# Two PSUM rows, an earlier fold and a whole load in the tail of a 2-D prefix-sum kernel

One Trainium2 chip, one core of it. The metric is the device time of one execution in microseconds (us); lower is better. A difference counts as faster or slower from 2% on.

## The reference

```python
def reference(x):                      # x: 4 x 4224 x 4224, float32
    ps = np.cumsum(np.cumsum(x, axis=1), axis=2)
    diag = np.diagonal(ps, axis1=1, axis2=2)
    return np.cumsum(diag, axis=1).astype(np.float32)
```

The output is small (4 x 4224), but every element of x above or below a diagonal place counts for some result, so all 285 MB have to be read.

## The kernel before

The kernel streams x in groups of 384 rows (three rows in each of 128 partitions, 6336 KB a load) through three buffers. ScalarE (ACT) sums rows left of the diagonal, VectorE (DVE) adds rows into column sums `u`, and TensorE (PE) gathers the column sums into a PSUM tile `d`. The last 384 rows of the last image come in two parts: part a (256 rows, two loads) and part b (128 rows, five small loads), so that little is left to do when the last bytes land. The change lies in this tail, and in how the group called 8 of the last image is loaded.

```python
# last image, groups 8 and 9: three loads each
for i, g in enumerate((LG - 2, LG - 1)):
    strip = strip_tile()
    for q in range(F):
        load(out=strip[:, q, :], in_=rows_of(b, g)[:, q, :])
    # ... act_sum and pair_sum of row sums, masked block, matmuls into d
    add_to(rsum[:, k, :], more[:, i, :])
# ...
matmul(carry_ps, earlier, pu, start=True)
matmul(carry_ps[:, 1:2], apart, pu[:, 0:1])
if not whole:
    sum_a(1, cp, c1, cp + 768)                     # part a, first piece: ACT and DVE
    for c in range(c0, cp, 256):                   # 768 columns folded to 256 by PE
        matmul(fold_a, ident, part_a[:, :, c : c + 256], start=c == c0)
# ... two scans on DVE, write-out of the other groups
sum_a(3, *acuts[1], acuts[1][0] + 640)             # part a, second piece
row_sums(asum[:, :, 5], fold_a)                    # "the fold": DVE reads PSUM
row_sums(arows, asum)
# ...
weigh_b(dtot[:, 2:3], weights, M0, start=True)     # fin_b: places 256 to 383
for h in range(2):
    weigh_a(arows[:, h : h + 1], h * P, start=h == 0)      # fin_a: places 0 to 255
for h in range(2):
    weigh_b(arows[:, h : h + 1], weights, h * P)
for k, ca in ((0, 416), (1, 416), (2, 416)):       # part b: ACT and DVE, three quarters
    act_sum(bsum[:, k, 0:1], part_b[:, k, :ca])
    pair_sum(bsum[:, k, 1:2], part_b[:, k, ca:])
    if k == 1:
        finish(fin_a, 0, M0)                       # yl = fin_a + c12
# ... weigh_b of bsum, three sums of the last quarter (esum), their matmuls (fin_e)
finish(fin_b, M0, GW)
# ... yl written out; ye = fin_e + yl, written out
```

In the code, `arows` holds the finished row sums of part a, the operand of its weighted sums `fin_a` and `fin_b`; `yl` and `ye` are the last outputs. Each engine takes its instructions in this order.

Of the kernel before, what the change touches and what calls it, by code (L numbers as in the profile page):

```python
# [8 lines left out]
FP32 = mybir.dt.float32  # L9
# [8 lines left out]
def kernel(  # L18
# [17 lines left out]
    nc = tc.nc  # L36
# [3 lines left out]
    P = 128  # L40
    F = 3
    GW = P * F
    NG = N // GW
    LB = B - 1
    LG = NG - 1
# [13 lines left out]
    psum_s = ctx.enter_context(  # L59
        tc.tile_pool(name="psum_s", bufs=1, space=bass.MemoryType.PSUM)  # L60
    )
# [6 lines left out]
    src = x[LB, T0:N, :].rearrange("(h p) w -> p h w", p=P)  # L68
# [4 lines left out]
    def strip_tile():  # L73
        return strips.tile([P, F, N], FP32, name="strip")

    def rows_of(b, g):

        return x[b, g * GW : (g + 1) * GW, :].rearrange("(p f) w -> p f w", f=F)

    load = nc.gpsimd.dma_start  # L80
# [17 lines left out]
    for um, pattern, cm in (  # L98
# [5 lines left out]
            out=um,  # L104
            in_=um,
# [12 lines left out]
        out=ident,  # L118
        in_=ident,
# [6 lines left out]
    def counted(name, rows, width, pieces):  # L126

        ti = consts.tile([P, GW], I32, name="counted")[:rows, :width]
        for c0, c1, base, step, cm in pieces:
            nc.gpsimd.iota(  # L130
                ti[:, c0:c1],
                pattern=[[step, c1 - c0]],
                base=base,
                channel_multiplier=cm,
            )
        tf = consts.tile([rows, width], FP32, name=name)
        nc.gpsimd.tensor_copy(out=tf, in_=ti)
        return tf
# [6 lines left out]
    def between_groups(name, n, turned):  # L145
# [37 lines left out]
    weights = counted("weights", P, GW, [(0, GW, 1, 1, -1)])  # L183
    nc.gpsimd.affine_select(
        out=weights,
        in_=weights,
# [8 lines left out]
    R = P // 4  # L195
# [3 lines left out]
        out=steps, in_=steps, scalar=2, op=ALU.arith_shift_right  # L199
    )  # L200
    weights4 = consts.tile([P, P], FP32, name="weights4")
    nc.vector.tensor_scalar_max(out=weights4, in0=steps, scalar1=0.0)

    def matmul(o, lhsT, rhs, start=False):
        nc.tensor.matmul(  # L205
            o, lhsT=lhsT, rhs=rhs, start=start, stop=False, skip_group_check=True
        )

    def act_sum(acc, src):

        nc.scalar.activation(out=src, in_=src, func=ACT.Copy, accum_out=acc)  # L211

    def row_sums(acc, src):
        nc.vector.reduce_sum(out=acc, in_=src, axis=AX.X)  # L214

    def pair_sum(acc, src):

        w = src.shape[-1] // 2
        pair = dumpool.tile([P, 896], FP32, name="pair")
        nc.vector.scalar_tensor_tensor(  # L220
            out=pair[:, :w],
            in0=src[:, :w],
            scalar=1.0,
            in1=src[:, w:],
            op0=ALU.mult,
            op1=ALU.add,
            accum_out=acc,
        )

    def add_to(o, i):  # L230
        nc.vector.tensor_add(out=o, in0=o, in1=i)  # L231

    def masked(o, i, m, acc):
        nc.vector.scalar_tensor_tensor(  # L234
            out=o,
            in0=i,
            scalar=1.0,
            in1=m,
            op0=ALU.mult,
            op1=ALU.mult,  # L240
            accum_out=acc,
        )
# [10 lines left out]
    asum = last.tile([P, 2, 6], FP32, name="asum")  # L253
    dtot = last.tile([P, F], FP32, name="dtot")
# [13 lines left out]
    for b in range(B):  # L268
        whole = b < LB
        if b in (0, LB):  # L270
            rows = NG if b else NW
# [4 lines left out]
        def row_of(j):  # L276
            return b * NG + j if whole else (j + 1) % NG

        def columns(j, rhs):

            k = row_of(j)
            matmul(d, sel[:, NW - 1 - k : NW - 1 - k + rows], rhs, start=first[0])
            first[0] = False

        def u_of(j):
            return u[:, j * GW : (j + 1) * GW]

        for g in range(NG if whole else LG - 2):
            strip = prefetched.pop(0) if prefetched else None
            if strip is None:  # L290
                strip = strip_tile()
                load(out=strip, in_=rows_of(b, g))  # L292
            k, lo, hi = row_of(g), g * GW, (g + 1) * GW
# [16 lines left out]
        if not whole:  # L310


            for j in range(LG - 2, NG):
                columns(j, u_of(j))
            columns(LG, head[:, 0, :])
            more = last.tile([P, 2, F], FP32, name="more")
            wa = 2176
            for i, g in enumerate((LG - 2, LG - 1)):
                k, lo, hi = row_of(g), g * GW, (g + 1) * GW
                strip = strip_tile()  # L320
                for q in range(F):
                    load(out=strip[:, q, :], in_=rows_of(b, g)[:, q, :])  # L322
                for q in range(F):
                    act_sum(rsum[:, k, q : q + 1], strip[:, q, :wa])
                    pair_sum(more[:, i, q : q + 1], strip[:, q, wa:hi])
                    block = strip[:, q, lo:hi]
                    masked(block, block, um3[:, q, :], rabove[:, k, q : q + 1])
                    for j in range(g + 1, NG):
                        columns(j, strip[:, q, j * GW : (j + 1) * GW])
                    columns(g, block)  # L330
                add_to(rsum[:, k, :], more[:, i, :])
# [8 lines left out]
        if not whole:  # L340

            strip = strip_tile()
# [7 lines left out]
            for sb, c0, c1 in (  # L350
# [6 lines left out]
                r0 = TB + sb * R  # L357
                load(  # L358
                    out=part_b[:, sb, c0:c1],
                    in_=x[b, r0 : r0 + R, :NH].rearrange("r (k c) -> r k c", k=4)[  # L360
                        :, :, c0:c1
                    ],
                )

            def sum_a(k, c0, c1, ca):
                for h in range(2):
                    act_sum(asum[:, h, k : k + 1], part_a[:, h, c0:ca])
                for h in range(2):
                    pair_sum(asum[:, h, k + 1 : k + 2], part_a[:, h, ca:c1])


            c0, c1 = acuts[0]
            cp = c0 + 768
            fold_a = psum_s.tile([P, 2, 256], FP32, name="fold_a")
# [3 lines left out]
        c12 = last.tile([rows, 2, GW], FP32, name=f"c12{rows}")  # L378
# [12 lines left out]
        for i, src in enumerate((d, c12[:, 0, :])):  # L391
            nc.vector.tensor_tensor_scan(  # L392
                out=c12[:, i, :],
# [6 lines left out]
        if whole:  # L400
# [5 lines left out]
            out=out[b, :T0].rearrange("(g i) -> g i", i=GW), in_=c12[1:, 1, :]  # L406
        )


        sum_a(3, *acuts[1], acuts[1][0] + 640)  # L410
        row_sums(asum[:, :, 5], fold_a)
        arows = last.tile([P, 2], FP32, name="arows")
        row_sums(arows, asum)


        M0 = 2 * P
        E0 = GW - R
        fin_a = psum_s.tile([1, M0], FP32, name="fin_a")
        fin_b = psum_s.tile([1, P], FP32, name="fin_b")
        fin_e = psum_s.tile([1, R], FP32, name="fin_e")  # L420
        yl = last.tile([1, GW], FP32, name="yl")

        def weigh_a(rows, r0, start=False):

            matmul(fin_a[:, r0:], rows, weights[:, : M0 - r0], start=start)

        def weigh_b(rows, w, r0, start=False):
            lo = max(r0, M0)
            matmul(fin_b[:, lo - M0 :], rows, w[:, lo - r0 : GW - r0], start=start)

        def finish(src, c0, c1):
            nc.vector.tensor_add(
                out=yl[:, c0:c1], in0=src, in1=c12[0:1, 1, c0:c1]
            )

        weigh_b(dtot[:, 2:3], weights, M0, start=True)
        for h in range(2):
            weigh_a(arows[:, h : h + 1], h * P, start=h == 0)
        for h in range(2):
            weigh_b(arows[:, h : h + 1], weights, h * P)  # L440


        bsum = last.tile([P, 3, 2], FP32, name="bsum")
        for k, ca in ((0, 416), (1, 416), (2, 416)):
            act_sum(bsum[:, k, 0:1], part_b[:, k, :ca])
            pair_sum(bsum[:, k, 1:2], part_b[:, k, ca:])
            if k == 1:
                finish(fin_a, 0, M0)
        for k in range(3):
            for i in (1, 0):  # L450
                weigh_b(bsum[:, k, i : i + 1], weights4, M0 + k * R)


        esum = last.tile([P, 3], FP32, name="esum")
# [2 lines left out]
        pair_sum(esum[:, 2:3], part_b[:, 3, bcut:])  # L457
        for k in (1, 0, 2):
            matmul(fin_e, esum[:, k : k + 1], weights4[:, :R], start=k == 1)
        finish(fin_b, M0, GW)  # L460
        nc.sync.dma_start(
            out=out[b, T0 : T0 + E0].unsqueeze(0), in_=yl[:, :E0]
        )
# [33 lines left out]
```

## Time and profile before

| | before |
|---|---|
| median of the first three runs, us | 670.92 (670.73 to 671.5) |
| span of the profiled run, us | 669.8 |
| bytes moved, mean rate | 285.61 MB, 426 GB/s |
| busy: PE, DVE, ACT | 13%, 67%, 40% |
| mean granted PE clock | 0.908 |

The DMA queue is full for the whole span, so only the few microseconds after the last landings can be shortened. The mean granted clock turns out to be worth reading: one stretch of 3.41 us at half clock lowers it by 3.41 x 0.5 / 669.8 = 0.0025. The mean granted PE clock of 0.908 is 119.4 us at half clock (from 523.5 to 642.9) and one stretch of 3.41 us in the tail.

### The profile page before, as it was taken

To read this page: it belongs to the slowest core of one execution; us is meant where nothing else is said; L and a number is where in the kernel's file an instruction comes from. 1 tells how busy PE (TensorE), PEld (TensorE's weight loads), DVE (VectorE), ACT (ScalarE), POOL (GpSimd) and SP (SyncE) were. 2 spreads that over 40 slices of the span, in tenths; PEclk is the share of its full clock that TensorE was granted. 3 is DMA by queue.
4 is the path that set the end of the run, shared out by engine and by line. 5 is a ranking of instruction groups with operands and counts; after the bars stand their busy time and mean duration, and the time that the engine had idled before them with its cause. 6 is when DMAs were issued, how large, how long until landed. Compare 5 with 4: busy or idle time off the path is not lost.

```text
span 669.8 us, 1147 instructions
## 1 busy us (share of the span) xinstructions
PE 84.9 (13%) x174; PEld 16.4 (2%) x174; DVE 450.1 (67%) x287; ACT 264.9 (40%) x251; POOL 36.1 (5%) x83
## 2 busy tenths in 40 slices
PE   0000110000010110000001000000002011000085
PEld 0000000000000000000000000000000000000022
DVE  3779866544398877655437988765442999876555
ACT  0012344556602333445661223344566122334743
POOL 5000000000000000000000000000000000000020
PEclk9999999999999999999999999999999655555588
DMA  9999999999999999999999999999999999999996
GB/s 371 436 436 436 436 436 436 430 436 433 433 427 418 430 436 436 433 433 436 436 433 436 436 433 436 436 424 418 427 436 436 430 436 436 436 436 416 425 423 266
DMA packets 8155, 285.61 MB, mean 426 GB/s; under 512 B 904, under 2 KB 1332, under 8 KB 1876
## 3 DMA queue, kind: packets, MB, share of 16 engines
q0 software_dynamic: 7680, 284.89, 98.7%
q1 hardware_dynamic: 468, 0.66, 0.3%
q14 instruction: 6, 0.05, 0.0%
q8 instruction: 1, 0.02, 0.0%
HBM read 285.47 MB, written 0.07 MB: 426 GB/s over the span
## 4 chain that ended last, share of the span: by engine, by line
DMA 66%; ACT 16%; DVE 14%; issue 2%; PE 1%; POOL 0%; ACTq 0%; DVEq 0%; POOLq 0%
DMA strip<-in_x_dram 66%; ACT strip L211 16%; DVE u L231 5%; DVE u L303 3%; DVE strip L300 2%; DVE above L214 2%; DVE sums L214 1%; PE d L205 0%; PE fin_b L205 0%; DVE c L392 0%; PE fin_a L205 0%; DVE pair L220 0%; POOL strip L347 0%; ACTq L211 0%; DVE asum L214 0%
## 5 line engine op out<-in xcount | busy, mean ns | idle before, releaser
L211 ACT ACTIVATE strip<-strip 128x768 f32<-128x768 f32 (+13 forms) x125 | 259.3, 2075 | 400.4 <-DMA strip<-in_x_dram 374.8
L231 DVE TENSOR_TENSOR u<-u,strip 128x3840 f32<-128x3840 f32 (+10 forms) x115 | 292.2, 2541 | 2.7
L300 DVE TENSOR_TENSOR strip<-strip,um 128x1152 f32<-128x1152 f32 x41 | 55.7, 1358 | 183.1 <-ACT strip L211 182.9
L205 PE MATMUL d<-u,sel 128*33 128x384 f32 (+1 forms) x88 | 64.6, 844 | 575.7 <-DVE u L231 575.7
L214 DVE TENSOR_REDUCE above<-strip 128x3 f32<-128x1152 f32 x41 | 55.5, 1353 | 1.4
L292 POOL DMA_DIRECT2D strip<-in_x_dram x38 | 20.2, 530 | 560.2 <-DVE u L231 504.2
L205 PEld LDWEIGHTS d<-u,sel 128*33 128x33 f32 (+1 forms) x88 | 8.0, 136 | 629.9 <-DVE u L231 626.9
L211 ACT ACTIVATION_READ_ACCUMULATOR strip<-strip 128x1 f32 x125 | 23.3, 186 | 0.0
L303 DVE TENSOR_TENSOR u<-strip 128x4224 f32<-128x4224 f32 x4 | 18.2, 4549 | 0.0
L220 DVE SCALAR_TENSOR_TENSOR pair<-strip 128x640 f32<-128x640 f32 (+6 forms) x15 | 9.8, 657 | 8.8 <-DMA strip<-in_x_dram 8.6
L205 PE MATMUL d<-strip,sel 128*11 128x384 f32 x30 | 10.0, 486 | 0.6 <-DVE strip L234 0.6
L214 DVE TENSOR_REDUCE sums<-strip 128x3 f32<-128x1152 f32 x4 | 5.4, 1341 | 7.0 <-DMA strip<-in_x_dram 7.0
L198 DVE TENSOR_SCALAR steps<-steps 128x128 int32<-128x128 int32 x1 | 0.2, 227 | 7.0 <-POOL steps L197 7.0
L322 POOL DMA_DIRECT2D strip<-in_x_dram x6 | 3.1, 529 | 27.4 <-issue 27.4
L214 DVE TENSOR_REDUCE pu<-d 33x1 f32<-33x384 f32 (+1 forms) x2 | 1.1, 548 | 3.6 <-PE d L205 3.6
L234 DVE SCALAR_TENSOR_TENSOR strip<-strip,um 128x384 f32<-128x384 f32 x6 | 3.3, 558 | 0.2
L358 POOL DMA_DIRECT2D strip<-in_x_dram x5 | 2.7, 552 | 4.9 <-DMA strip<-in_x_dram 4.9
L205 PE MATMUL fold_a<-strip,ones_all 128*128 128x512 f32 x6 | 2.8, 610 | 0.8 <-DMA strip<-in_x_dram 0.8
L205 PEld LDWEIGHTS d<-strip,sel 128*11 128x11 f32 x30 | 2.7, 93 | 7.7 <-issue 6.0
L205 PE MATMUL d<-ones_all,r 128*33 128x128 f32 (+1 forms) x12 | 2.3, 346 | 0.1
L347 POOL DMA_DIRECT2D strip<-in_x_dram x2 | 1.4, 709 | 13.2 <-issue 13.2
L392 DVE TENSOR_TENSOR_SCAN c<-ones_all,carry,c 33x384 f32<-33x384 f32 (+1 forms) x2 | 2.0, 1008 | 0.1
(73 smaller groups left out, 36.9 us busy)
## 6 DMA issues: line engine op xcount, KB each, us to landing
strip<-in_x_dram POOLq DMA_DIRECT2D x41, 6336.0 KB, 27.7
strip<-in_x_dram POOLq DMA_DIRECT2D x6, 2112.0 KB, 22.3
strip<-in_x_dram POOLq DMA_DIRECT2D x1, 2304.0 KB, 18.9
strip<-in_x_dram POOLq DMA_DIRECT2D x1, 1536.0 KB, 22.0
strip<-in_x_dram POOLq DMA_DIRECT2D x3, 480.0 KB, 23.1
head<-in_x_dram SPq DMA_DIRECT2D x1, 576.0 KB, 3.9
strip<-in_x_dram POOLq DMA_DIRECT2D x1, 352.0 KB, 23.8
strip<-in_x_dram POOLq DMA_DIRECT2D x1, 128.0 KB, 19.3
```

Of the source, the lines that this page charges most:

```text
L205: nc.tensor.matmul(o, lhsT=lhsT, rhs=rhs, start=start, stop=False, skip_group_check=True)
L211: nc.scalar.activation(out=src, in_=src, func=ACT.Copy, accum_out=acc)
L214: nc.vector.reduce_sum(out=acc, in_=src, axis=AX.X)
L220: nc.vector.scalar_tensor_tensor(out=pair[:, :w], in0=src[:, :w], scalar=1.0, in1=src[:, w:], op0=ALU.mult, op1=ALU.add, accum_out=acc,)
L231: nc.vector.tensor_add(out=o, in0=o, in1=i)
L234: nc.vector.scalar_tensor_tensor(out=o, in0=i, scalar=1.0, in1=m, op0=ALU.mult, op1=ALU.mult, accum_out=acc,)
L292: load(out=strip, in_=rows_of(b, g))
L300: nc.vector.tensor_mul(out=block, in0=block, in1=um3)
L303: nc.vector.tensor_add(out=u, in0=strip[:, 0, :], in1=strip[:, 1, :])
L322: load(out=strip[:, q, :], in_=rows_of(b, g)[:, q, :])
L358: load(out=part_b[:, sb, c0:c1], in_=x[b, r0 : r0 + R, :NH].rearrange("r (k c) -> r k c", k=4)[:, :, c0:c1],)
L392: nc.vector.tensor_tensor_scan(out=c12[:, i, :], data0=ones_row[:rows], data1=src, initial=carry[:, i : i + 1], op0=ALU.mult, op1=ALU.add,)
```

## The change

The intent is a shorter tail: the fold is reduced while DVE is idle; part a's weighted sums get a row of their own over all 384 places (two matmuls in place of four), so that nothing of part a stands between part b and its row; and group 8 needs one load in place of three.

```diff
-                for q in range(F):
-                    load(out=strip[:, q, :], in_=rows_of(b, g)[:, q, :])
+                if g == LG - 2:
+                    load(out=strip, in_=rows_of(b, g))
+                else:
+                    for q in range(F):
+                        load(out=strip[:, q, :], in_=rows_of(b, g)[:, q, :])
 ...
+        row_sums(asum[:, :, 5], fold_a)
         sum_a(3, *acuts[1], acuts[1][0] + 640)
-        row_sums(asum[:, :, 5], fold_a)
 ...
-        fin_a = psum_s.tile([1, M0], FP32, name="fin_a")
+        fin_a = psum_s.tile([1, GW], FP32, name="fin_a")
 ...
-        weigh_b(dtot[:, 2:3], weights, M0, start=True)
-        for h in range(2):
-            weigh_a(arows[:, h : h + 1], h * P, start=h == 0)
-        for h in range(2):
-            weigh_b(arows[:, h : h + 1], weights, h * P)
+        weigh(fin_a, arows[:, 0:1], weights, 0, True)
+        weigh(fin_a, arows[:, 1:2], weights, P)
+        weigh(fin_b, dtot[:, 2:3], weights, 0, True)
 ...
-                finish(fin_a, 0, M0)
+                nc.vector.tensor_add(out=yl, in0=fin_a, in1=c12[0:1, 1, :])
 ...
-        finish(fin_b, M0, GW)
+        add_to(yl[:, M0:], fin_b)
```

More of the change, by code (lines that the diff above doesn't have):

```diff
@@ L421, with weigh @@
         yl = last.tile([1, GW], FP32, name="yl")
-        def weigh_a(rows, r0, start=False):
-            matmul(fin_a[:, r0:], rows, weights[:, : M0 - r0], start=start)
-        def weigh_b(rows, w, r0, start=False):
-            lo = max(r0, M0)
-            matmul(fin_b[:, lo - M0 :], rows, w[:, lo - r0 : GW - r0], start=start)
-        def finish(src, c0, c1):
-            nc.vector.tensor_add(
-                out=yl[:, c0:c1], in0=src, in1=c12[0:1, 1, c0:c1]
-            )
-        weigh_b(dtot[:, 2:3], weights, M0, start=True)
-        for h in range(2):
-            weigh_a(arows[:, h : h + 1], h * P, start=h == 0)
-        for h in range(2):
-            weigh_b(arows[:, h : h + 1], weights, h * P)
+        def weigh(o, rows, w, r0, start=False):
+            n = o.shape[-1]
+            matmul(o[:, r0:], rows, w[:, : n - r0], start=start)
+        weigh(fin_a, arows[:, 0:1], weights, 0, True)
+        weigh(fin_a, arows[:, 1:2], weights, P)
+        weigh(fin_b, dtot[:, 2:3], weights, 0, True)
         bsum = last.tile([P, 3, 2], FP32, name="bsum")
@@ L447 @@
             if k == 1:
-                finish(fin_a, 0, M0)
+                nc.vector.tensor_add(out=yl, in0=fin_a, in1=c12[0:1, 1, :])
         for k in range(3):
             for i in (1, 0):
-                weigh_b(bsum[:, k, i : i + 1], weights4, M0 + k * R)
+                weigh(fin_b, bsum[:, k, i : i + 1], weights4, k * R)
         esum = last.tile([P, 3], FP32, name="esum")
```

## The prediction

> **What bounds the kernel now.** I read the page first (sections 1, 2 and 4), then the chain of waits over the last 80 us, then the timeline of ACT around group 8, and last the windows of a quarter of a microsecond over the tail.
>
> ```profile
> PEclk9999999999999999999999999999999655555588
> DMA  9999999999999999999999999999999999999996
> ...
> DMA 66%; ACT 16%; DVE 14%; issue 2%; PE 1%; POOL 0%; ACTq 0%; DVEq 0%; POOLq 0%
> ```
> The DMA row is 9 in every slice but the last. The page gives 285.61 MB moved at a mean of 426 GB/s over the span of 669.8 us, and most slices move 433 to 436. No engine comes near: DVE 67%, ACT 40%, PE 13% busy. The ACT and DVE shares in the chain are waits for a free buffer that run while an earlier load is still arriving; they cost nothing. So the time is the load stream plus what is left to do after the last bytes. Only the second part, and the efficiency of the stream itself, can move.
>
> Chain of waits, 590 to 670 us:
> ```profile
> 639.03 21.96 DMA strip<-in_x_dram
> ...
> 661.01 0.64 DVE pair L220 x2
> ...
> 661.68 0.63 DVE pair L220 x2
> ...
> 662.31 0.62 DVE asum L214
> ...
> 663.05 0.18 DVE arows L214
> ...
> 663.27 1.34 PE fin_a L205 x4
> 664.62 2.58 PE fin_b L205 x16
> ...
> 667.22 0.29 DVE yl L432
> ...
> 667.60 0.18 DVE ye L465
> ```
> The reader is to see that the chain leaves the DMA at 660.99, when the second piece of part a lands, though the last piece of part b lands only at about 666.2. From there it is DVE (two pair sums, the fold, arows), then PE without a pause from 663.27 to 667.20, then two adds and the write-out. The last pair sum of part b (666.28, 0.29 us, accumulator at 666.58) is off the chain: PE is still at its queue then. So in this execution PE ends the kernel, by some 0.5 us over the data.
>
> The windows tell why PE is late (columns: window; its length, then busy time and count of PE, PEld, DVE, ACT, POOL; granted clock; DMA share; GB/s):
> ```profile
> 663.00:663.25 0.25, 0.00 (x0) 0.00 (x0) 0.20 (x2) 0.09 (x2) 0.00 (x0) 1.00 0.97 375
> 663.25:663.50 0.25, 0.23 (x1) 0.09 (x2) 0.25 (x2) 0.07 (x1) 0.00 (x0) 0.80 0.60 219
> 663.50:663.75 0.25, 0.25 (x2) 0.13 (x1) 0.22 (x3) 0.25 (x1) 0.00 (x0) 0.50 0.36 135
> ...
> 666.75:667.00 0.25, 0.25 (x6) 0.24 (x4) 0.00 (x0) 0.00 (x0) 0.00 (x0) 0.87 0.00 0
> ```
> The clock falls to half at about 663.4, just as PE begins its last work, and comes back at about 666.8. Nearly all of the tail's matmuls run at half speed.
>
> **What the Trainium skill says.** "TensorE: Matmul & The Clock Gate", section "What's actually happening": the array runs at half clock after an idle window of about 3.4 us, at full clock after a busy one, and the window runs free, so its phase differs between executions. The trace agrees: half clock from 663.4 to 666.8 is 3.4 us, and 643.0 (where it rose before) lies six such windows earlier. "DMA: Bandwidth & Descriptors", section "Anatomy of one DMA — SWDGE (gpsimd) path": a fixed part of about 2 us per transfer beside bytes at 436 GB/s. The rate agrees (436 in most slices); the fixed part does not show in the stream, because loads queue behind one another: the thirds of groups 8 and 9 land 4.97 to 5.14 us apart, three of them in 15.1 us, against 15.00 for a whole group. "PSUM — Partial Sum Buffer", section "PSUM bank collisions raise a hardware error": accesses of two engines have to be kept apart by bank. No run here shows it; I only note that a row of 384 fp32 fits a bank as a row of 256 does, so the change needs no more banks.
>
> **The change part by part.**
>
> *Group 8 whole.* Three issues of 2112 KB become one of 6336 KB. In the timeline of ACT the first sums of groups 5, 6, 7 start at 591.40, 606.39, 621.39, hence 15.0 us a load; the last third of group 8 starts at
> ```profile
> 636.47 2.02 ACT L211 ACTIVATE strip<-strip 128x2176 f32<-128x2176 f32 x1 [2.72 <-DMA strip<-in_x_dram]
> ```
> that is 15.08 after group 7, and group 9's thirds at 641.61, 646.58, 651.63, 15.16 in all. So whole saves about 0.08 us of the stream, if it is not noise. Against that, ACT loses its early start on the first two thirds: three sums of 2.02 plus 0.19 less their overlap, some 6.4 us, from 636.47 to about 642.8. Group 9's first third lands at 641.6, so it waits 1.2 us and is done at about 645; its second third lands at 646.5. The delay dies there. DVE loses nothing on the blocks: in the kernel before it was busy with group 7 until 637.69 and took all of group 8 after that anyway; only its small add of the sums now waits for ACT to 642.8 instead of 641.73, again gone before 646.5. Sum: -0.1 us, plus nothing.
>
> *The fold first.* The scan ends at 660.53 and DVE idles 0.49 us until 661.01. The fold's reduce (0.69 us) fills that idle time: it runs 660.55 to 661.24, PE having ended its matmuls at 660.08. The two pair sums (0.62 and 0.08 each, 1.22 together in the chain) then end at about 662.5 instead of 662.31. The ACT sums of the same piece end at 662.57. So arows starts at about 662.65, bound by ACT, not at 663.05: 0.4 us earlier. That is the largest gain, and it is at the head of the chain.
>
> *The rows of PSUM.* An fp32 matmul shows as two instructions. PE after arows, in columns streamed: before 2 x (256 + 128) for fin_a, 2 x (128 + 128) for fin_b, 2 x 2 x (128 + 96 + 64) = 1152 for part b: 2432. After: 2 x (384 + 256) = 1280, and the dtot matmul, which used to run at 660.02 in idle time, now behind arows: 256, and 1152: 2688. Two matmuls fewer in the list, but 256 columns more on the path. At half clock two fin_b instructions of 128 columns take 0.42 us (starts 664.41 and 664.83), so 1.66 ns a column; at full clock half of it, 0.83. Issue counts earn nothing here, since the weight loads (0.13 us) lie beside the streams (0.21 us). Cost: 0.42 us cold, 0.21 us warm.
>
> *The adds.* The first add to yl grows from 256 to 384 columns: 0.41 us for 256 and 0.28 for 128 give 0.13 per 128, so 0.55 us. It sits in the DVE queue ahead of the third pair sum. The last one stays 128 wide, 0.28 us.
>
> *The sum, at the clock phase of this profile.* PE starts at 662.9. Until 663.43 it is warm: 0.53 us, 640 columns. The other 640 of part a take 1.06 us, to 664.5; the add runs 664.55 to 665.1, so pair sum three moves from 664.99 to 665.1, done by 665.6, in time for the next piece. dtot to 664.9, part b to about 666.85 (half clock to the end), against 667.20. The three matmuls of fin_e then need the last sum at 666.58, and end at about 667.1. End: 0.3 us earlier, with the stream's 0.1 some 0.35.
>
> **The rivals.** (1) *It is the data that ends it.* If the window's phase lets PE stay at full clock, the 2432 columns before take 2.0 us and end at 665.3 without waits; then both kernels hang on the last sum at 666.58 and end alike, about 0.4 us below this profile. The timed runs (670.73, 670.92, 671.5; the profiled one 671.49) spread by 0.77 us, which such a phase could explain. Gain then: 0 to 0.1 us. (2) *PE gets worse.* If the clock falls before 662.9, all 2688 columns run cold until the window ends: part a to 665.0, the wide add to 665.6, and the pair sums of part b slide behind it by 0.3 to 0.6 us; the end is then level with before, or 0.2 us later. The dtot matmul no longer breaks PE's idle stretch (660.08 to 662.9), which speaks a little for it; the gap being shorter than the 3.4 us window speaks against. (3) *The whole load hurts the stream*, for ACT starts later, or frees a buffer late. The final strip takes the buffer of group 7, not of group 8, which speaks against; it would show as a gap in the DMA row near 640 us, and cost at most the 1.2 us by which ACT is late.
>
> **Range and chances.** Taking the three phases as about equally likely, the gain is 0.1 to 0.4 us, 0.2 in the mean: 670.92 - 0.2 = 670.7. The runs' own spread of 0.77 us is larger than the effect, so 670.0 to 671.4. Two per cent is 13.4 us; nothing in the change reaches a stage of that size, since the stream of 285 MB is the same.
>
> **What would show each step.** Right: DMA row unchanged and group 8 landing 15.0 us after group 7; the fold's reduce at about 660.6 and arows at about 662.65; fin_a taking some 0.5 us more than before for the same clock; dtot's matmul behind it; the first add 0.55 us. Wrong: arows still at 663.0 (ACT or a semaphore holds it), a pause of DVE for the wide add with the last sums after 666.9, or loads landing later than 15.0 us apart. If the span moved by over 1 us, the stream itself would have changed, and this reasoning would be at fault.

## The result, and the profile after

The changed kernel took 671.17 us (median of four fast runs: 670.92, 671.05, 671.29 and 672.45); the kernel before took 670.95 in the same rounds (670.73 to 671.5). The ratio is 1.0006, 95% interval 0.9988 to 1.0023: the same. Ratios here are the mean time of one kernel's fast runs over that of the other's of the same rounds, so not quite the ratio of the medians quoted.

The page of the kernel after, sections 2 and 4:
```profile
PEclk9999999999999999999999999999999999999998
DMA  9999999999999999999999999999999999999996
...
DMA 67%; ACT 16%; DVE 13%; issue 3%; PE 1%; POOL 0%; ACTq 0%; DVEq 0%; POOLq 0%
```
The DMA row is the one of before. The clock row is not: the long half-clock stretch of before is missing. That is a matter of the record, not of the clock. The packed trace of this execution holds no clock record before 641.7 us, and time without a record counts as full. PE's work from 530 to 630 us, before and after (columns as in the prediction):
```profile
530.00:630.00 100.00, 10.18 (x14) 0.80 (x14) 79.16 (x33) 38.53 (x43) 5.78 (x11) 0.50 1.00 430
530.00:630.00 100.00, 10.18 (x14) 0.80 (x14) 79.23 (x33) 38.27 (x42) 4.74 (x9) 1.00 1.00 432
```
The same 14 matmuls took the same 10.18 us, under "0.50" and under "1.00". So mean clocks of 0.908 and 0.997 tell the same of the tail: one half-clock stretch. What differs is the phase of the clock's steps, 663.4 before and 662.1 after; so the two tails can't be subtracted from each other.

DVE in the kernel after (start, length, engine, line, operation; idle time before it and its releaser):
```profile
660.35 0.66 DVE L214 TENSOR_REDUCE asum<-fold_a 128x2 f32<-128x512 f32 x1
...
662.54 0.17 DVE L214 TENSOR_REDUCE arows<-asum 128x2 f32<-128x12 f32 x1 [0.33 <-ACT strip L211]
...
665.09 0.55 DVE L441 TENSOR_TENSOR yl<-fin_a,c 1x384 f32<-1x384 f32 x1 [1.26 <-PE fin_a L205]
665.57 0.42 DVE L220 SCALAR_TENSOR_TENSOR pair<-strip 128x272 f32<-128x272 f32 x1
```
The fold fills the idle time and arows waits for ACT alone, as forecast. The wide add takes 0.55 us, as forecast. But DVE sits idle for 1.26 us until fin_a is there, with the third pair sum queued behind the add. PE's side of it:
```profile
662.76 2.29 PE L205 MATMUL fin_a<-weights,arows 128*1 128x384 f32 x4 [2.79 <-DVE arows L214]
664.85 0.64 PE L205 MATMUL fin_b<-weights,dtot 128*1 128x128 f32 x2
```
From 662.76 to 664.85 is 2.09 us for 1280 columns, 1.63 ns each: half clock from the first matmul on. In the windows of half a microsecond the clock is 1.00 up to 662.00, 0.64 in the next window and 0.50 after it, so it fell at about 662.1. This is the second of the prediction's rivals.

Group 8's first sum on ACT starts at 636.45, 14.99 us after group 7's (15.08 before).

### The profile page after: what moved, and what is told of

Read it like the earlier page. It is cut to its first block, busy times and chain, and to the rows that moved or that the text cites. A ratio compares the mean times of both kernels' runs of the same rounds, so it can differ in the third digit from the quotient of the medians.

```text
span 669.2 us, 1137 instructions
## 1 busy us (share of the span) xinstructions
PE 84.3 (13%) x170; PEld 15.7 (2%) x170; DVE 450.1 (67%) x287; ACT 264.8 (40%) x251; POOL 35.0 (5%) x81
## 4 chain that ended last, share of the span: by engine, by line
DMA 67%; ACT 16%; DVE 13%; issue 3%; PE 1%; POOL 0%; ACTq 0%; DVEq 0%; POOLq 0%
DMA strip<-in_x_dram 67%; ACT strip L211 16%; DVE u L231 5%; DVE u L303 3%; DVE strip L300 2%; DVE above L214 2%; DVE sums L214 1%; PE d L205 0%; DVE c L395 0%; POOL strip L361 0%; POOL strip L350 0%; DVE pair L220 0%; ACTq L211 0%; DVE pu L214 0%; DVE c L234 0%
## 5 line engine op out<-in xcount | busy, mean ns | idle before, releaser
L292 POOL DMA_DIRECT2D strip<-in_x_dram x38 | 20.2, 530 | 560.3 <-DVE u L231 504.3
L361 POOL DMA_DIRECT2D strip<-in_x_dram x5 | 2.7, 548 | 4.7 <-DMA strip<-in_x_dram 4.7
L205 PE MATMUL fin_a<-weights,arows 128*1 128x384 f32 (+1 forms) x4 | 2.3, 729 | 2.8 <-DVE arows L214 2.8
L325 POOL DMA_DIRECT2D strip<-in_x_dram x3 | 1.6, 530 | 14.2 <-issue 14.2
L350 POOL DMA_DIRECT2D strip<-in_x_dram x2 | 1.4, 710 | 13.2 <-issue 13.2
```

Of the source, the lines that this page charges most:

```text
L205: nc.tensor.matmul(o, lhsT=lhsT, rhs=rhs, start=start, stop=False, skip_group_check=True)
L292: load(out=strip, in_=rows_of(b, g))
L350: load(out=part_a[:, :, c0:c1], in_=src_a[:, :, c0:c1])
L361: load(out=part_b[:, sb, c0:c1], in_=x[b, r0 : r0 + R, :NH].rearrange("r (k c) -> r k c", k=4)[:, :, c0:c1],)
```

## The experiments

All runs below were correct against the reference. In each group the kernel before ran in the same rounds on the same chip. The theory at first was that the gains and losses of the parts cancel; the rivals are given with each run.

### One part at a time

**The changed kernel again**, with no edit.

> The changed kernel once more, unaltered. Theory 1 (the parts cancel: the earlier fold gains up to 0.4 us, the 256 columns and the wider add lose as much): 670.6 to 671.2 us, ratio to the kernel before within 0.1%. Theory 2 (the phase of the PE clock's window sets each run): the same median, but single runs spread by some 0.7 us in both kernels, and the profile's tail is longer the sooner the clock falls before arows. Rival (the change is truly slower, by the whole load or the wide add): 0.3 us or more above before in all rounds.

Measured: 672.3 us (672.01 to 672.89, five runs), before 671.03 (670.83 to 671.37, nine runs), ratio 1.0021, interval 1.0007 to 1.0035. A miss of both theories, and outside the range of my prediction: here the changed kernel is truly slower, by about 0.2%, as the rival had it; which part does it is for the next runs.

**The fold first, alone:**
```diff
+        row_sums(asum[:, :, 5], fold_a)
         sum_a(3, *acuts[1], acuts[1][0] + 640)
-        row_sums(asum[:, :, 5], fold_a)
```

> The kernel before with only the fold's reduce put ahead of the two pair sums. Theory 1: arows starts 0.4 us sooner after the landing of part a's second piece (1.6 us behind it in place of 2.05), the time falls by 0.1 to 0.35 us: 670.6 to 670.8. Rival (the last bytes of part b end it, not PE): arows as early, but the time is the same within 0.1 us.

Measured: 672.33 us (670.96 to 672.64), ratio 1.0015, interval 1.0003 to 1.0028. The part from which I expected the largest gain makes four of five runs slower; the fifth took 670.96.

**The two PSUM rows, alone** (the fold and group 8 as before):

> The changed kernel with the fold in its old place and group 8 in thirds again: only the two PSUM rows are new. Theory 1: PE's columns after arows grow from 2432 to 2688, and the wide add (0.55 us) holds the third pair sum of part b back; 0.2 to 0.5 us slower than before where the clock is at half, 0 where it is full: 671.0 to 671.4. Rival (two matmuls fewer count, columns do not): 0.1 to 0.2 us faster than before.

Measured: 671.08 us, ratio 1.0005, interval 0.9992 to 1.0017; four runs between 670.94 and 671.09, one of 672.65, whose cause is not known. In the profile taken, the tail ran at full clock, where 0 was expected.

**Group 8 whole, alone:**

> The kernel before with only group 8 loaded whole. Theory 1: group 8 lands 15.0 us after group 7 and not 15.08, ACT's lateness is gone before the second third of group 9 lands; the time falls by 0.1 us or not at all: 670.8 to 671.0. Rival (ACT's delay of 1.2 us is passed on): the scans end later than 0.1 us before part a's second piece lands, and the time rises by up to 1 us.

Measured: 670.93 us (670.62 to 671.18), ratio 0.9999, interval 0.9986 to 1.0011. In agreement with 0.1 us or nothing; the runs don't resolve it. ACT's lateness was not passed on: arows starts 2.04 us after part a's second piece, as before.

The profile of the repeated changed kernel shows what fold first does. Chain of waits, 635 to 675 us:
```profile
657.21 4.55 PE fold_a L205 x6
...
661.78 0.69 DVE asum L214
662.48 0.55 DVE pair L220 x2
```
DVE's timeline of the same run:
```profile
661.78 0.69 DVE L214 TENSOR_REDUCE asum<-fold_a 128x2 f32<-128x512 f32 x1 [1.29 <-PE fold_a L205]
...
663.81 0.17 DVE L214 TENSOR_REDUCE arows<-asum 128x2 f32<-128x12 f32 x1
```
In the profiles of before and after, PE took 2.84 us for the fold:
```profile
657.24 2.84 PE L205 MATMUL fold_a<-strip,ones_all 128*128 128x512 f32 x6 [0.76 <-DMA strip<-in_x_dram]
```
Here it takes 4.55, because the clock was at half from 658.2 to 661.6. The Trainium skill, "Perfetto Trace Analysis", section "Tensor Engine Instruction (MATMUL, LD_WEIGHTS)", says that ACT and DVE take their instructions strictly in order. The trace agrees: the pair sums' data had landed by 660.97 (ACT started on them then), yet DVE stood still for 1.29 us, 0.81 of them after that landing, until the fold that now stands ahead of them was there. arows starts at 663.81, 2.84 us after the landing, in place of 2.04 in the old order.

In the old order a late fold costs nothing. The profile of the two rows alone happened to have the same slow fold (4.54 us, from 657.42 to 661.96), but there the pair sums kept DVE busy until 662.4, and the fold's reduce began at 662.40 with no wait:
```profile
657.42 4.54 PE L205 MATMUL fold_a<-strip,ones_all 128*128 128x512 f32 x6 [0.76 <-DMA strip<-in_x_dram]
...
662.40 0.69 DVE L214 TENSOR_REDUCE asum<-fold_a 128x2 f32<-128x512 f32 x1
```

That explains 0.8 us of delay in arows, but why does the end slip as much? The windows of 3.41 us, laid along the steps of the clock, show it (columns as in the prediction). The repeated changed kernel:
```profile
654.77:658.18 3.41, 1.45 (x10) 0.66 (x8) 1.98 (x6) 0.91 (x3) 0.00 (x0) 1.00 1.01 416
658.18:661.59 3.41, 3.41 (x5) 0.98 (x3) 2.24 (x5) 1.47 (x4) 0.00 (x0) 0.50 1.03 415
661.59:665.00 3.41, 1.12 (x5) 0.34 (x5) 2.84 (x10) 2.47 (x9) 0.00 (x0) 1.00 0.54 212
665.00:668.41 3.41, 3.08 (x22) 2.05 (x19) 2.04 (x9) 0.81 (x4) 0.00 (x0) 0.50 0.01 5
```
And the two rows alone, at nearly the same phase, with the old order:
```profile
657.84:661.25 3.41, 3.41 (x5) 1.35 (x4) 2.82 (x8) 1.47 (x5) 0.00 (x0) 0.50 1.03 415
661.25:664.66 3.41, 1.92 (x8) 0.45 (x7) 2.78 (x10) 2.66 (x8) 0.00 (x0) 1.00 0.69 272
664.66:668.07 3.41, 1.91 (x21) 1.08 (x18) 1.96 (x9) 1.18 (x4) 0.00 (x0) 1.00 0.03 12
668.07:669.30 1.23, 0.00 (x0) 0.00 (x0) 0.00 (x0) 0.00 (x0) 0.00 (x0) 0.51 0.00 0
```
The first PE number of each row goes with the clock of the row below it. With the old order arows comes early enough for PE to be busy 1.92 us of the third window, and the tail keeps its full clock. With the fold first arows comes late, PE is busy only 1.12 us of that window, and the next one, with all the last matmuls, runs at half. So the delay seems to bring its own slow clock with it. The other pair of profiles with a slow fold agrees: 1.44 us and then half with the fold first alone, 1.90 us and then full with the fold put back (below). But busy time is not the exact measure: the last two rows have 1.91 us followed by half clock, and in the long-fold run below 1.61 us was followed by full. Which windows count as idle is thus known only at the ends (1.46 us and less, 1.92 and more), and the step from late arows to half clock is argued from these four profiles.

### The clock, and the lateness, apart from each other

The new theory: fold first is slow because of the clock. If so, it must cost nothing when PE is kept busy. Three places get matmuls of constants into an unused PSUM bank (the same edit on three kernels):
```diff
+            fill = psum_s.tile([P, 512], FP32, name="fill")
+            def keep_busy(*widths):
+                for n in widths:
+                    matmul(fill[:, :n], ident, ones_all[:, :n], start=True)
+            keep_busy(512)          # before the carry matmuls
 ...
+            keep_busy(256)          # between these and the fold
 ...
+        keep_busy(512, 512, 256)    # behind the fold, ahead of the weighted sums
```

> The kernel before with the fold first, and with idle matmuls into an unused bank that keep PE busy before, between and after the fold's own. New theory (the fold's six instructions take 4.54 us in place of 2.84 when the clock's window has fallen to half before them; DVE, which now asks for the fold first, stands still for it 1.3 us): with PE kept busy the fold takes 2.84 us in every run, arows starts some 1.6 us after part a's second piece lands, and all five runs lie at 670.3 to 670.8, none near 672.3. Rival (fold first is slow for another reason, such as the DVE read of that bank or a wait on ACT): the slow runs near 672.3 stay.

Measured: 670.94 us (670.83 to 671.0), before 671.16 (670.79 to 672.41, nine runs), ratio 0.9992, interval 0.998 to 1.0005. No slow run in five; the median is 0.14 us above the range expected.

> The changed kernel with the same idle matmuls. New theory: the clock is at full in the whole tail, the fold takes 2.84 us, 2688 columns take 2.2 us, the last pair sum ends the kernel: 670.3 to 670.8 us in all five runs. Rival (the wide add and the PSUM rows are slower in themselves): 0.2 us or more above the kernel before with the same idle matmuls.

Measured: 670.75 us (670.62 to 670.93), ratio 0.9989, interval 0.9976 to 1.0003.

> The kernel before with the same idle matmuls. New theory: its runs lose the spread (670.83 to 671.5) and lie at 670.3 to 670.8, as the data end it. Rival (PE's clock does not matter, or the idle matmuls stand in the way of the real ones): 671.0 or more.

Measured: 670.93 us (670.82 to 671.12), ratio 0.9993, interval 0.998 to 1.0005: the spread went, at a level just above the range expected. So at full clock the three kernels lie within 0.2 us of each other: the rows, the wide add and the fold's place hardly matter then. The chain of waits of the changed kernel with these matmuls:
```profile
646.97 19.30 DMA strip<-in_x_dram
...
666.36 0.31 DVE pair L220 x2
...
666.72 0.23 PE fin_e L205 x2
...
666.98 0.18 DVE ye L467
```
The last data now end the kernel, and PE only follows.

**A late fold at full clock.** To tell the lateness from the clock, the fold's first matmul is done three times (the repeats start the sum anew, so the result is the same), in the old order and in the new:
```diff
-            for c in range(c0, cp, 256):
+            for c in (c0, c0, c0, c0 + 256, c0 + 512):
```

> The kernel before with the fold's first matmul done three times (the repeats are overwritten, the result is the same): at full clock PE ends the fold 1.7 to 1.9 us later, about as late as the half-clock fold did. New theory (the old order hides a late fold behind the two pair sums, which run until 662.3): asum starts at most 0.3 us later where the clock is full, time 670.9 to 671.3. Rival (any delay of the fold is passed on): 672.5 or more.

Measured: 671.33 us (670.88 to 673.01), before 671.22 (670.9 to 671.91, nine runs), ratio 1.0002, interval 0.999 to 1.0015.

> The same longer fold with the reduce of the fold first. New theory: DVE stands still for the fold by some 1.3 to 1.5 us even where the clock is full, arows starts at about 664, and the time is 672.0 to 672.7 in nearly all runs, 1 us or more over before_longfold. Rival (the fold's place in the queue does not matter, the slow runs come from the clock in the later matmuls): within 0.3 us of before_longfold.

Measured: 671.56 us (670.89 to 673.55), ratio 1.0009, interval 0.9995 to 1.0022. The stall came as expected (1.31 us, arows at 663.84 and not 663.01), but the time did not: the difference of the medians is 0.23 us, not 1. In its profile the clock stayed full to the end, and the span is 669.2 us, as with the old order:
```profile
661.81 0.69 DVE L214 TENSOR_REDUCE asum<-fold_a 128x2 f32<-128x512 f32 x1 [1.31 <-PE fold_a L205]
...
666.86 0.18 DVE L465 TENSOR_TENSOR ye<-fin_e,yl 1x32 f32<-1x32 f32 x1
```
So my theory was too simple. A late arows alone is absorbed; the time is lost where the clock falls in the tail as well. The single runs of both long-fold kernels fit: the six with no half-clock stretch in the tail by their mean clock (0.911 or 1.000) took 670.88 to 671.56, the four with one (0.997) took 671.62 and 673.01 in the old order, 672.59 and 673.55 in the new. So a half-clock stretch seems to cost something in either order.

**The fold put back**, with the rows and the whole load kept:

> The changed kernel with only the fold's reduce put back behind the pair sums (PSUM rows and whole group 8 stay). New theory: the slow runs near 672.3 that the changed kernel has go away; 670.8 to 671.2, with at most one run above. Rival (rows or the whole load make the slow runs): most runs stay at 672 or more.

Measured: 671.29 us (670.61 to 671.85), ratio 0.9998, interval 0.9984 to 1.0011. No run reached 672, where six of the changed kernel's nine had; but three lie over 671.2, more than I expected, so this removes the worst runs and no more.

**A version against both.** The changed kernel with the idle matmuls, and two things more:
```diff
+        weigh(fin_b, dtot[:, 2:3], weights, 0, True)
         weigh(fin_a, arows[:, 0:1], weights, 0, True)
         weigh(fin_a, arows[:, 1:2], weights, P)
-        weigh(fin_b, dtot[:, 2:3], weights, 0, True)
 ...
-            if k == 1:
+            if k == 2:
                 nc.vector.tensor_add(out=yl, in0=fin_a, in1=c12[0:1, 1, :])
```

> The changed kernel with idle matmuls that keep PE's clock up, the dtot matmul ahead of arows, and the wide add behind the third pair sum. New theory: the data end it in every run, so it can't be under after_warm by more than 0.1 us: 670.5 to 670.9, 0.3 us under the kernel before. Rival (the wide add or the dtot matmul still cost): 0.2 us or more under after_warm's 670.75.

Measured: 670.71 us (670.62 to 670.86), before 671.22 (670.9 to 671.91), ratio 0.999, interval 0.9977 to 1.0002. All five runs lie under all nine of before, but the gain of some 0.5 us is 0.1%, and the interval just includes 1. It is no better than the idle matmuls alone.

### All in one table

Times after the landing of part a's second piece, taken as the start of ACT's sum of 640 columns, so that differences in the stream drop out. "arows" and "end" are the starts of the arows reduce and of the last add (ye) on DVE.

| profile | half clock at | arows, us | end, us |
|---|---|---|---|
| before | last matmuls (from 663.4) | 2.04 | 6.59 |
| group 8 whole alone | last matmuls (from 662.4) | 2.04 | 6.22 |
| after | last matmuls (from 662.1) | 1.64 | 6.16 |
| rows alone | fold | 2.04 | 5.87 |
| fold put back | fold | 2.04 | 5.67 |
| after, repeated | fold and last matmuls | 2.84 | 7.20 |
| fold first alone | fold and last matmuls | 2.84 | 7.39 |
| before, idle matmuls | nowhere | 2.04 | 5.88 |
| fold first, idle matmuls | nowhere | 1.64 | 5.88 |
| after, idle matmuls | nowhere | 1.64 | 5.85 |
| before, long fold | nowhere | 2.04 | 5.88 |
| fold first, long fold | nowhere | 2.86 | 5.88 |
| after, idle matmuls, wide add later | nowhere | 1.63 | 5.83 |

At full clock the end does not follow arows: it may start anywhere from 1.63 to 2.86 us and the end stays at 5.83 to 5.88. With the last matmuls at half clock the end is later, 6.16 to 6.59 us with arows at 1.64 to 2.04, and 7.20 to 7.39 with arows at 2.84. How much of that last step is the late arows and how much the later place of the half-clock window is not separated: no profile has a late arows and half clock in the last matmuls alone.

### Thirds in the whole stream

```diff
-                load(out=strip, in_=rows_of(b, g))
+                for q in range(F):
+                    load(out=strip[:, q, :], in_=rows_of(b, g)[:, q, :])
```

> The changed kernel with every load after the first three (save the final strip's) in thirds: 39 more loads split than in the changed kernel. If a split costs the 0.08 us that I read from group 8, the time rises by 3.1 us to about 674.5 (or 675.5 with the slow fold). If splits cost nothing in a full queue: 671 to 672.5 as the changed kernel. Rival (early thirds let ACT and DVE free the buffers sooner and the stream runs better): below 670.9.

Measured: 678.27 us (677.79 to 680.05, four runs), ratio 1.0106, interval 1.009 to 1.0122. The edit splits 38 more loads than the changed kernel has split (the text says 39, which is the count with group 9), so 37 more than before: (678.27 - 671.16) / 37 = 0.19 us each, twice what I read from group 8. The GB/s rows of the two pages, first the kernel before:
```profile
GB/s 371 436 436 436 436 436 436 430 436 433 433 427 418 430 436 436 433 433 436 436 433 436 436 433 436 436 424 418 427 436 436 430 436 436 436 436 416 425 423 266
```
and with thirds:
```profile
GB/s 370 434 429 429 427 427 427 429 427 427 428 426 429 429 427 427 427 428 429 426 427 429 428 427 426 427 429 429 427 427 426 431 427 425 428 428 442 418 421 245
```
The plateau falls from 436 to 427 to 429, with the queue as full as before; but the slices of 418 to 424 within the plateau of before are gone too, and the mean falls only from 426 to 422. The packets for the same bytes rise from 8155 to 18812, so the cost may lie with the packets and not with the split as such; no run separates the two.

## Why the prediction was right, and where it was not

The forecast of 670.7 us, within 2%, held in its range at the first comparison (671.17, in 670.0 to 671.4). Its sign did not: it said 0.2 us faster, and the changed kernel was level there and 1.3 us slower in the repeat. That the first comparison fell inside the range was luck in part: by their mean clocks, three of its four runs had one half-clock stretch, while four of the five runs of the repeat had two.

- **The stream bounds it:** right. No version but the one with thirds moved more than 2 us in the median, and that one because it changed the stream.
- **Group 8 whole, -0.1 us:** right in size as far as it could be seen (14.99 us for 15.08; alone 670.93 for 671.03). The cost of a split was read too small: 0.19 us on average over the stream, where group 9's thirds (0.16) were the better sample. That ACT's lateness dies was right.
- **The fold first, -0.4 us at the head of the chain: the step that failed.** The -0.4 holds at full clock (arows 1.64 us after the landing in place of 2.04). It rested on "PE having ended its matmuls at 660.08", a full-clock fold. At half clock the fold ends some 1.7 us later, DVE waits for it, and arows starts 0.8 us later than in the old order. I let the clock vary over the last matmuls and forgot that it varies over the fold too.
- **256 more columns and the wide add:** right as arithmetic (1280 columns in 2.09 us, the add 0.55 us). The changed kernel and group 8 whole alone, both with the clock falling at 662.1 to 662.4, end alike (6.16 and 6.22 us), though arows is 0.4 us sooner in the first. That fits the loss I worked out, but it is one pair of profiles. At full clock the rows cost nothing visible.
- **The phases as equally likely, with the gain averaged over them:** wrong. The sum is wrong too: its three phases give 0.35, 0 to 0.1 and 0 to -0.2 us, hence 0.1 in the mean and not 0.2, and the range of 0.1 to 0.4 leaves out its own second rival. That PE's gap is "shorter than the 3.4 us window" was no argument against that rival: in the profile after PE stood idle for 2.79 us before fin_a, and the clock fell 2.17 us into that gap. The phase varies from run to run, but how busy PE is in a window depends on the kernel. Fold first lets PE idle longer after a slow fold, and that seems to bring on the second half-clock window. The clocks of single runs agree: 9 of the 14 runs with the fold first (changed kernel and fold first alone) show two such stretches (0.906, or 0.995), against 4 of 42 in the old order (before where its clock is on record, rows alone, group 8 alone, fold put back). Of the changed kernel's nine runs, the three at 0.997 took 670.92 to 671.29, and the five with two stretches 672.01 to 672.59.

Open: the changed kernel's slowest run (672.89) had a mean clock of 0.908, so one stretch and not two. The kernel before has such runs too (671.36 to 672.41), and the rows alone one of 672.65 at 0.997. No profile fell on one of these, so what they lose is not shown. Over all rounds 2 of 31 runs of before took over 672 us, and 6 of 9 of the changed kernel.

## What to carry to other kernels

An instruction moved ahead in an in-order queue is safe only if its input is early in every state of the producer; here the start of arows gained 0.4 us in one clock state and lost 0.8 in the other. Where PE works in short bursts near the end, read at which clock each burst ran before pricing a reorder, and look at the mean granted clock of single runs, after checking from which time on the clock is on record: profiles at different phases can't be subtracted. A few idle matmuls that keep PE's window busy took the slow runs away (20 runs of four kernels, none over 671.12 us), though no gain was clear of noise; reordering the work only shifted them.

## What the Trainium skill lacked or had wrong

- "TensorE: Matmul & The Clock Gate", section "What's actually happening", speaks of an idle window but not of how idle. Here a window of 3.41 us with PE busy for 1.12 or 1.45 us was followed by half clock, and one with 1.92 us by full clock. Over the recorded windows of all 14 profiles, cut at each run's own clock steps, 1.46 us and less led to half and 1.92 and more to full; between 1.61 and 1.91 both occur. PE need not idle a whole window through: in the kernel after it had been idle for 2.17 us (from 659.97) when the clock fell at 662.14.
- "DMA: Bandwidth & Descriptors", section "Anatomy of one DMA — SWDGE (gpsimd) path", gives about 2 us fixed per transfer. In a full queue two more transfers of the same bytes cost 0.19 us together (37 more groups in thirds than before, 426 to 422 GB/s in the mean); no page found gives the cost of splitting a queued load.
- No page found says from which time the clock is on record. Here the records begin at 640.8 to 644.0 us in 11 of 14 profiles, and the time before reads as full clock, though the same matmuls took 10.18 us there in both readings.
